# Weights alone on SyncE's queue, other transfers on GpSimd's, forms made in steps, layer-two gates kept on chip, last sums by transfers: a two-layer decoder trunk on one core

## The chip, the core and the metric

The kernel runs on one core of a Trainium2 chip. The core has five engines with queues of their own: TensorE (PE in the profile; its weight loads are PEld), VectorE (DVE), ScalarE (ACT), GpSimd (POOL) and SyncE (SP). Each executes its own instructions in order and waits for the others at semaphores. SyncE and GpSimd issue the DMA transfers here. The metric is the time of the program on the device in microseconds; the median of several runs counts.

## The reference

The input x has 512 rows (positions) of 2048 columns, in fp32. It passes two layers. Each is a token mixer with a gate, and then a residual sum with a LayerNorm.

```python
def fox_branch(x, w_in, b_f, q_gain, k_gain, w_out):          # layer 0, 16 heads of 128
    proj = jnp.einsum('bsd,de->bse', x, w_in)                 # 2048 -> 4*2048 + 16
    q, k, v, gate, f_logit = jnp.split(proj, [...], axis=-1)
    q = rms_norm(heads(q), q_gain); k = rms_norm(heads(k), k_gain); v = heads(v)
    c = jnp.cumsum(jax.nn.log_sigmoid(f_logit + b_f), axis=1).transpose(0, 2, 1)
    s = q k^T * scale + c[..., :, None] - c[..., None, :]     # causal, in blocks of 128 rows
    o = softmax(s) v
    return jnp.einsum('bse,ed->bsd', o * jax.nn.silu(gate), w_out)

def retention_branch(x, w_in, w_out):                         # layer 1, 8 heads, qk 256, v 512
    q, k, v, gate = jnp.split(jnp.einsum('bsd,de->bse', x, w_in), [...], axis=-1)
    q = rotary(q); k = rotary(k) * 256 ** -0.5
    o = (q k^T * decay) v                                     # written in the reference by chunks
    o = group_norm_heads(o)
    return jnp.einsum('bse,ed->bsd', o * jax.nn.silu(gate), w_out)

def reference(x, ...):
    h = x
    for i in range(2):
        y = fox_branch(...) if i % 2 == 0 else retention_branch(...)
        h = layer_norm(4.0 ** 0.25 * h + y, ln_gain[i], ln_bias[i])
    return h
```

## The kernel before

**Products.** All projections are products of a 512 x 2048 activation with slabs of weights: "narrow" slabs of 512 columns (q and k of two heads of layer one, or of one head of layer two) and "wide" ones of 1024 columns (gate and values, or half of an output projection). A `Unit` (L164) does one slab by a two-by-two scheme with seven products, p1 to p7, in place of eight. On the activation's side the products take seven *forms* (L40): the quarters a11, a12, a22 and the sums s1 to s4 of quarters. On the side of the weights they take quarters or running sums of quarters. Each fp32 operand is split into a high part (`w_h`, a rounded copy on ScalarE, L143) and a low part (`w_l`, the difference, on VectorE, L144), and `mm3` (L146 to 150) does three matmuls for one product.

**Blocks.** A weight quarter comes in blocks of 512 KB: two for a narrow unit, four for a wide one, so that a unit has 14 or 28 blocks in its seven products. For each block `run` (L263) loads it on SyncE (`load`, L181; tag `st`, three buffers, or a chain tile q0 to q3 that is kept), adds it to the chain or to another block where the product needs a sum (VectorE, L199 and L202), splits it (w_h and w_l have three buffers each), and queues the matmuls, which run two blocks behind the splits (`ahead`, `advance(2)`). `after` (L241) joins the products: it keeps p1, p5 and u2 in SBUF (tags k0 to k2) and hands four finished quarters to a `sink`.

**Work between blocks.** The mixers are lists of small steps in `pending` (L104). After the matmuls of each block `tick` runs one or more steps of that list, so that the heads of one unit are worked on between the blocks of the next. `finish_pending` runs all that is left at once. The order of the instructions on an engine follows their dependences and readiness, not strictly this text.

**Layer one.** `begin` (L285) does p1 and p2 of the first narrow and the first wide unit; meanwhile `form_of_x` and `combine` (L301) make the forms of x, all of them before `finish_pending` returns (L622). `forget` makes the cumulated logarithms. For each pair of heads: `scale` and `turn` (L473 to 496) normalise q and k, and for each head eight steps (L500 to 580): four row blocks of scores with a softmax (`cb`, the row of c, is loaded at L511), the transposes, `by_head` loads of values and gates (L538), mix, and gate. `give` (L344) then writes the head's result y, with signs by the table `GIVES`, into the forms of the output projection in DRAM: plain stores on SyncE (L356), accumulating transfers on GpSimd (L354). Heads 14 and 15 write their parts of the forms on chip (`last_heads`). `fetch_form` (L358) reads forms back and splits them, through the `st` buffers.

**The passage.** Units 4 and 5 are the output projection of layer one, the second in the order `EARLY`. `add_z` (L672) loads a block of x (tag tmp, four buffers, L83), adds and takes LayerNorm's statistics. `to_columns` (L715) normalises a row block, stores it (`z_norm`) and queues `turn` (L695), four transposes with gain and bias into the quarters of the new activation. After unit 5 the pipeline is drained (L735), the last turns are queued with `combine`, and `begin` starts layer two.

**Layer two.** Per head: `take_qk` copies q and k out, `attend` (L758) rotates them (two `cos_sin` tables, L768) and makes decayed scores (`dec`, L781), and two steps `residual` (L852) prepare alpha times the normalised row for later: three loads, two VectorE instructions, one store. `take_vg` (L795) writes the gate to DRAM (`rgates`, L607) and splits the values. `retain` (L804) queues mix, mix, norm, turn, turn twice: the mix reads the gate back (L816), the turn scales it (L832), transposes it (L835) and gives y and its negative to the forms.

**Output.** Units 14 and 15 add the first half of the output projection to the residual (`add_half`, L877: load, add, store), 16 and 17 the second; `store` (L896) does the last LayerNorm, every second column block with a sum on GpSimd (L904).

## Time and profile before

| | |
|---|---|
| Median of 3 runs | 2582.72 us (2579.68 to 2583.9) |
| The profiled execution's own time | 2578.53 us |
| Its span, from the first to the last instruction | 2576.8 us |
| Mean granted TensorE clock | 0.964 |
| Instructions | 34,299 |
| Read from HBM / written | 430.33 MB / 75.27 MB |

The profile is of one execution. A busy engine's row gives microseconds, share of the span and the number of instructions. A group's row gives line, engine, operation, what it writes and reads, shapes and count; then total busy time and the mean of one in ns; then the engine's idle time just before and what ended it. A row of waits names who waited at which line, for whom, with total us, count and the longest. A row of windows gives busy time and instructions of each engine, the clock granted to TensorE, the mean busy share of 16 DMA engines and GB/s. A row of issues gives the transfer, the issuing queue, the count, the size and the median us from issue to landing. `q0` is the queue of GpSimd's transfers, `q1` that of SyncE's.

### The profile page before, as it was taken

The numbers are of one execution on the slowest core, as the hardware profiler recorded it, in microseconds if no ns is written. First come the engines' busy times: TensorE is split into PE (matmuls) and PEld (weight loads), VectorE is DVE, ScalarE is ACT, GpSimd is POOL, SyncE is SP. The second block draws the span as 40 slices with busy tenths as digits, with TensorE's granted clock in tenths as the row PEclk, the third lists the DMA queues.
The fourth block names the chain that finished last, engine by engine and source line by source line (L and its number), as shares of the span: only waits on it lengthen the run. The fifth ranks groups of instructions, "written<-read, shape, count | busy, mean of one in ns | idle before, by whom it ended". The sixth has DMA issues, their size and how long they took to land.

```text
span 2576.8 us, 34299 instructions
## 1 busy us (share of the span) xinstructions
PE 2349.0 (91%) x12820; PEld 2001.7 (78%) x12820; DVE 2004.3 (78%) x2617; ACT 1276.9 (50%) x1891; POOL 100.8 (4%) x116
## 2 busy tenths in 40 slices
PE   6899999999997898699999999999999988897994
PEld 5788898898886687579797878788888866675773
DVE  7778687777776779887878878787878788577778
ACT  5456566666566445444454444444544444343432
POOL 0000000001101000000000000000000100100001
PEclk8999999999998999899999999999999999999997
DMA  6465746645755657467566566666676666677564
GB/s 243 156 217 168 235 150 172 217 160 159 221 190 162 217 188 269 155 196 208 178 220 194 193 191 202 181 203 189 208 212 201 190 198 216 191 241 241 193 213 147
DMA packets 213159, 507.86 MB, mean 197 GB/s; under 512 B 20080, under 2 KB 76784, under 8 KB 212736
## 3 DMA queue, kind: packets, MB, share of 16 engines
q1 hardware_dynamic: 198592, 485.22, 56.9%
q0 software_dynamic: 14400, 20.45, 5.6%
q8 instruction: 100, 1.64, 0.3%
q14 instruction: 67, 0.55, 0.1%
HBM read 430.33 MB, written 75.27 MB: 196 GB/s over the span
## 4 chain that ended last, share of the span: by engine, by line
PE 24%; DVE 14%; DMA 11%; issue 4%; ACT 4%; SPq 0%; POOL 0%; ACTq 0%; POOLq 0%; DVEq 0%
PE acc L149 7%; PE acc L150 7%; PE acc L148 7%; DVE w_l L144 5%; DMA w_raw<-in_wide 4%; ACT w_h L143 3%; DVE w_raw L202 2%; DMA w_raw<-in_narrow 2%; DMA y_s<-ny 1%; DMA cos_sin<-in_rot 1%; DMA ln_g<-in_ln_g 1%; DVE w_raw L199 1%; PE mmp L148 1%; DMA gate<-rgates 1%; DMA y_raw<-y_s 1%
## 5 line engine op out<-in xcount | busy, mean ns | idle before, releaser
L143 ACT ACTIVATE w_h<-w_raw 128x1024 fp32r<-128x1024 f32 x728 | 762.7, 1057 | 919.0 <-PE acc L150 277.0
L144 DVE TENSOR_TENSOR w_l<-w_raw,w_h 128x1024 fp32r<-128x1024 f32 x728 | 882.9, 1220 | 285.5 <-ACT w_h L143 281.1
L148 PE MATMUL acc<-w_h,s 128*128 128x512 f32 (+1 forms) x1664 | 607.7, 365 | 50.6 <-ACT w_h L143 46.6
L149 PE MATMUL acc<-w_l,s 128*128 128x512 f32 (+1 forms) x1664 | 609.2, 366 | 21.2 <-DVE w_l L144 20.4
L150 PE MATMUL acc<-w_h,s 128*128 128x512 f32 (+1 forms) x1664 | 602.6, 362 | 0.0
L148 PE MATMUL acc<-w_h,a 128*128 128x512 f32 (+1 forms) x1248 | 459.8, 369 | 47.3 <-ACT w_h L143 34.6
L149 PE MATMUL acc<-w_l,a 128*128 128x512 f32 (+1 forms) x1248 | 456.4, 366 | 33.8 <-DVE w_l L144 33.8
L150 PE MATMUL acc<-w_h,a 128*128 128x512 f32 (+1 forms) x1248 | 453.6, 363 | 0.0
L202 DVE TENSOR_TENSOR w_raw<-w_raw 128x1024 f32<-128x1024 f32 x312 | 378.5, 1218 | 69.8 <-DMA w_raw<-in_narrow 34.3
L148 PEld LDWEIGHTS acc<-w_h,s 128*128 128x128 f32 x1664 | 318.7, 192 | 108.3 <-ACT w_h L143 58.5
L149 PEld LDWEIGHTS acc<-w_l,s 128*128 128x128 f32 x1664 | 319.2, 192 | 84.2 <-DVE w_l L144 40.1
L150 PEld LDWEIGHTS acc<-w_h,s 128*128 128x128 f32 x1664 | 319.2, 192 | 43.5 <-DVE s L144 0.4
L148 PEld LDWEIGHTS acc<-w_h,a 128*128 128x128 f32 x1248 | 241.7, 194 | 91.9 <-ACT w_h L143 42.4
L149 PEld LDWEIGHTS acc<-w_l,a 128*128 128x128 f32 x1248 | 241.7, 194 | 72.4 <-DVE w_l L144 38.7
L150 PEld LDWEIGHTS acc<-w_h,a 128*128 128x128 f32 x1248 | 241.5, 194 | 35.0
L199 DVE TENSOR_TENSOR w_raw<-w_raw 128x1024 f32<-128x1024 f32 x104 | 126.9, 1220 | 51.1 <-DMA w_raw<-in_wide 39.8
L148 PE MATMUL acc<-s,w_h 128*128 128x256 f32 x512 | 145.9, 285 | 5.1 <-DVE u L255 2.0
L149 PE MATMUL acc<-s,w_h 128*128 128x256 f32 x512 | 146.1, 285 | 0.0
L150 PE MATMUL acc<-s,w_l 128*128 128x256 f32 x512 | 146.0, 285 | 0.0
L148 PE MATMUL acc<-a,w_h 128*128 128x256 f32 x384 | 110.8, 288 | 1.0 <-DVE p L258 1.0
L149 PE MATMUL acc<-a,w_h 128*128 128x256 f32 x384 | 110.1, 287 | 0.0
L150 PE MATMUL acc<-a,w_l 128*128 128x256 f32 x384 | 109.9, 286 | 0.0
(187 smaller groups left out, 2558.3 us busy)
## 6 DMA issues: line engine op xcount, KB each, us to landing
w_raw<-in_wide SPq DMA_DIRECT2D x468, 512.0 KB, 4.0
w_raw<-in_narrow SPq DMA_DIRECT2D x200, 512.0 KB, 3.6
y_raw<-y_s SPq DMA_DIRECT2D x35, 256.0 KB, 4.1
gate<-rgates SPq DMA_DIRECT2D x32, 256.0 KB, 4.6
y_s<-ny POOLq DMA_DIRECT2D x32, 256.0 KB, 7.5
y_raw<-y_a SPq DMA_DIRECT2D x26, 256.0 KB, 4.0
y_a<-y SPq DMA_DIRECT2D x24, 256.0 KB, 3.0
y_s<-y POOLq DMA_DIRECT2D x24, 256.0 KB, 7.0
```

What stands on the lines that cost most here:

```text
L143: nc.scalar.activation(h, src, AF.Copy)
L144: nc.vector.tensor_sub(l, src, f32(h))
L148: nc.tensor.matmul(ps, a[0], b[0], start=start, stop=False, skip_group_check=True)
L149: nc.tensor.matmul(ps, a[0], b[1], start=False, stop=False, skip_group_check=True)
L150: nc.tensor.matmul(ps, a[1], b[0], start=False, stop=stop, skip_group_check=True)
L199: nc.vector.tensor_add(t, t, b)
L202: nc.vector.tensor_add(self.chain[c], self.chain[c], t)
```

## The change

SyncE's queue keeps the weight loads, the loads of x at the start and the stores of the output. All other transfers are issued by GpSimd: `give`'s plain stores, `fetch_form`, `cb`, `by_head`, the stores of gates and values of layer one, `cos_sin`, `dec`, the residual's loads and stores, `z_norm`, and the blocks of z.

- Forms are made in single steps between blocks. A set `awaited` names forms that are not done; `multiply` runs pending steps until the form it needs is there. The first units start without draining the pipeline before them, the wide one first in layer two. x comes in smaller pieces.
- The gate of a layer-two head stays in SBUF (in the kept p1 and in k2) until the mix. The scaling moves from `turn` into `norm`, and the four turns follow after both norms.
- In the two units with the order EARLY, the sums of p7 and p4 are made by accumulating transfers into the tile of the other block, in place of VectorE's additions.
- z blocks of units 5, 15, 16 and 17 are loaded up to three ahead. The last sums of `store` are all VectorE's. Forms are fetched through tiles of their own (k2, k0, u; g2; in0 and in1).
- tmp has three buffers in place of four; the narrow unit keeps p1 and p5 in one tile (k1) and u2 in `u`. `scale` works on half of the rows at a time, p7's subtraction on halves, and one p2 block of unit 4 moves behind p3 and p7. Part of `to_columns` and `turn` goes from VectorE to ScalarE.

```diff
-        [(p, 3) for p in ("p5", "p6", "p2")] + blocks_of(4, ("p3", "p7"), ("p4",)))
+        [(p, 3) for p in ("p5", "p6")] + blocks_of(4, ("p3", "p7")) + [("p2", 3)] + blocks_of(4, ("p4",)))
...
-        return pool.tile([P, 512], F32, name=name, tag="tmp", bufs=4)
+        return pool.tile([P, 512], F32, name=name, tag="tmp", bufs=3)
...
+            if (p, c) in self.summed:
+                return self.summed.pop((p, c))
...
+        def add_by_transfer(self, p, c, q, t):
+
+            nc.gpsimd.dma_start(t.rearrange("p a b -> p (a b)"), self.w[self.n, int(q[1]) - 1, int(q[0]) - 1, c],
+                                accum_op=ALU.add)
+            self.summed[p, c] = t
...
         def multiply(self, p, c, w, streamed):
+            while FORM[p] in awaited:
+                pending.popleft()()
...
                 self.keep("p5", "z")
+                if self.early:
+
+                    for i in range(2):
+                        t = pool.tile([P, 2, 2, 512], F32, name="v_sum", tag=HOME["s1"][i])
+                        for c in range(2):
+                            nc.sync.dma_start(t[:, c].rearrange("p a b -> p (a b)"), self.w[self.n, 1, 0, 2 * i + c])
+                            self.add_by_transfer("p7", 2 * i + c, "22", t[:, c])
...
-                nc.vector.tensor_sub(k["p5"], k["p5"], b["x"])
+                for e in range(2):
+                    nc.vector.tensor_sub(k["p5"][:, e], k["p5"][:, e], b["x"][:, e])
...
                 split(raw, *w)
+                if self.early and p == "p6":
+                    self.add_by_transfer("p4", c, "21", self.chain[c])
...
-        for u in (first, second):
-            u.run(BEGIN, streamed=True)
+        for i, u in enumerate((second, first) if wide_first else (first, second)):
+            u.run(BEGIN, streamed=u is second, **{k: v[i] for k, v in kw.items()})
...
+        def step(name, c, make, last=True):
+            if c == 0 and name not in made:
+                made.add(name)
+                new_form(name)
+            make(c)
+            if c == 1 and last:
+                awaited.discard(name)
...
+        steps = [partial(step, "s1", c, s1) for c in range(2)] + [partial(step, "s2", c, s2) for c in range(2)]
+        steps.append(lambda: (s4_sum(0), s4_sum(1)))
+        for name, f in (("s4", s4), ("s3", s3), ("a22", a22)):
+            steps += [partial(step, name, c, f) for c in range(2)]
+        return steps
...
-                nc.sync.dma_start(d, y if sign > 0 else ny)
+                nc.gpsimd.dma_start(d, y if sign > 0 else ny)
...
-            t = pool.tile([P, n, 256], F32, name="y_raw", tag="st", bufs=3)
+            t = pool.tile([P, n, 256], F32, name="y_raw", tag=tag, **(dict(bufs=3) if tag == "st" else {}))
...
                 for e in range(2):
-                    nc.sync.dma_start(t[:, :, e * P:(e + 1) * P], yf[i][name][:, e, c:c + n])
+                    nc.gpsimd.dma_start(t[:, :, e * P:(e + 1) * P], yf[i][name][:, e, c:c + n])
...
-    form_of_x("11")
-    nothing = lambda: None
-    pending.extend([partial(form_of_x, "12"), nothing, nothing, nothing, quarters_of_x] + combine())
-    begin(qk[0], vg[0])
-    advance(0)
-    finish_pending()
...
+    first = iter([partial(form_of_x, "11", (0, 2, 4)), partial(form_of_x, "11", (4, 8)),
+                  partial(form_of_x, "12", (0, 4)), partial(form_of_x, "12", (4, 8))])
+    start = lambda: next(first)()
+
+    def combined():
+        pending.extend(combine() + [forget])
+
+    begin(qk[0], vg[0], before=({i: start for i in range(4)},
+                                {i: partial(quarter_of_x, *at) for i, at in enumerate(
+                                    (("21", 0), ("22", 0), ("21", 1), ("22", 1)))}),
+          then=({}, {2: combined}), spread=(0, 14))
...
-                nc.sync.dma_start(at["cb"], fox["rows"][head:head + 1, :].to_broadcast([P, S]))
+                nc.gpsimd.dma_start(at["cb"], fox["rows"][head:head + 1, :].to_broadcast([P, S]))
...
-                nc.sync.dma_start(t, src[head // 4][:, :, js])
+                nc.gpsimd.dma_start(t, src[head // 4][:, :, js])
...
+        def load():
+            if todo:
+                s, c = todo.popleft()
+                there.append(sb2("z_in"))
+                nc.gpsimd.dma_start(there[-1], src(s, c))
...
-    Unit(wide, 5, partial(add_z, 1, ALPHA, x_rows)).run(EARLY, then={"p3": first_half})
-    advance(0)
-    finish_pending()
-    to_columns(2)
-    to_columns(3)
-    new_quarters(1)
-    pending.extend(combine())
+    sink, load = add_z(1, ALPHA, x_rows, True, EARLY)
+    Unit(wide, 5, sink).run(EARLY, then={0: load, "p3": first_half, "p4": second_half})
...
-                        nc.sync.dma_start(cs[i], rot[i])
+                        nc.gpsimd.dma_start(cs[i], rot[i])
...
             if n == 0:
-                to_rows(rgates[self.h], True, m, tile)
+                self.gates[m] = tile if m == 0 else pool.tile([P, 2, 512], F32, name="gate", tag="k2")
+                silu_twice(self.gates[m], tile)
                 return
...
-                g[q] = sb2("gate")
-                nc.sync.dma_start(g[q], rgates[self.h][:, q])
...
+                for e in range(2):
+                    nc.scalar.activation(g[2 * i + e], g[2 * i + e], AF.Copy, scale=r[i][:, e:e + 1])
...
-                nc.scalar.activation(g[q], g[q], AF.Copy, scale=r[q // 2][:, q % 2:q % 2 + 1])
...
-                pending.extend([partial(mix, 2 * i), partial(mix, 2 * i + 1), partial(norm, i),
-                                partial(turn, 2 * i), partial(turn, 2 * i + 1)])
+                pending.extend([partial(mix, 2 * i), partial(mix, 2 * i + 1), partial(norm, i)])
+            pending.extend(partial(turn, q) for q in range(ST))
...
-        nc.sync.dma_start(t, z_norm[s][:, cs])
+        nc.gpsimd.dma_start(t, z_norm[s][:, cs])
...
-        nc.sync.dma_start(z_res[s, c], t)
+        nc.gpsimd.dma_start(z_res[s, c], t)
...
-        then = fetch_while(1) if h.h == RH - 1 else {}
+        then = fetch_while(1, ("g2",)) if h.h == RH - 1 else {}
...
-            if c % 2:
-                nc.scalar.activation(z, z, AF.Copy, scale=r)
-                nc.gpsimd.tensor_add(z, z, gb[1][:, cs])
-            else:
-                nc.vector.scalar_tensor_tensor(z, z, r, gb[1][:, cs], op0=ALU.mult, op1=ALU.add)
+            nc.vector.scalar_tensor_tensor(z, z, r, gb[1][:, cs], op0=ALU.mult, op1=ALU.add)
```

More of the change, by code (lines that the diff above doesn't have):

```diff
@@ L320, in s4 @@
[L320 to L332 removed]
+        sl = lambda c: (slice(None), slice(4 * c, 4 * c + 4))
@@ L804, in retain @@
         def retain(self):
-            mv, r, g = {}, {}, {}
+            mv, r = {}, {}
+            g = [self.gates[q // 2][:, q % 2] for q in range(ST)]
             def mix(q):
```

290 lines of the change are left out of this document (171 added, 119 removed).

## The prediction

> **What bounds the kernel now.** I read the head of the page first: the span, the busy time of each engine, the granted TensorE clock.
>
> ```profile
> span 2576.8 us, 34299 instructions
> PE 2349.0 (91%) x12820; PEld 2001.7 (78%) x12820; DVE 2004.3 (78%) x2617; ACT 1276.9 (50%) x1891; POOL 100.8 (4%) x116
> PEclk8999999999998999899999999999999999999997
> L143 ACT ACTIVATE w_h<-w_raw 128x1024 fp32r<-128x1024 f32 x728 | 762.7, 1057 | 919.0 <-PE acc L150 277.0
> L202 DVE TENSOR_TENSOR w_raw<-w_raw 128x1024 f32<-128x1024 f32 x312 | 378.5, 1218 | 69.8 <-DMA w_raw<-in_narrow 34.3
> ```
>
> TensorE is the bound: it idles 2576.8 - 2349.0 = 227.8 us, and no edit removes a product. So the change can win back idle time, and the clock that goes with it. The 728 splits count the weight blocks: 2576.8 / 728 = 3.54 us a block on average, mixers included. Next I cut the span into windows: start, layer one, the passage from layer one to two, the heads of layer two, the last output units, the tail.
>
> ```profile
> core 0: us, PE busy (x) PEld busy (x) DVE busy (x) ACT busy (x) POOL busy (x), PEclk, DMA share, GB/s
> 0.00:150.00 150.00, 122.65 (x714) 106.06 (x715) 114.15 (x140) 75.43 (x112) 1.09 (x8) 0.95 0.56 193
> 150.00:750.00 600.00, 593.94 (x3769) 527.15 (x3767) 458.93 (x671) 378.57 (x756) 31.71 (x36) 1.00 0.61 189
> 750.00:1110.00 360.00, 303.01 (x1536) 250.28 (x1537) 286.30 (x421) 188.09 (x312) 6.97 (x8) 0.92 0.61 197
> 1110.00:2050.00 940.00, 894.21 (x4972) 772.51 (x4971) 749.84 (x944) 426.78 (x498) 38.34 (x45) 0.98 0.65 199
> 2050.00:2557.00 507.00, 435.14 (x1837) 345.71 (x1835) 381.31 (x410) 205.34 (x212) 16.46 (x16) 0.94 0.66 209
> 2557.00:2577.00 20.00, 0.00 (x0) 0.00 (x0) 13.74 (x35) 2.67 (x4) 6.24 (x4) 0.60 0.27 105
> ```
>
> The TensorE idle times are 27.4, 6.1, 57.0, 45.8, 71.9 and 20.0 us. The clock is below 1 just where idle time lies, so a stall costs more than its length: (1 - clock) x busy is 6.1, 0, 24.2, 17.9 and 26.1 us. Per microsecond of idle time that makes 0.22, 0, 0.42, 0.39 and 0.36 more, and I let a recovered microsecond bring that along (an estimate: the clock need not follow in proportion).
>
> Third, who ended those waits. The rows come from the list of TensorE's waits, asked window by window (row 1 is of 0 to 150, rows 2 to 4 of 750 to 1110, rows 5 to 7 of 1110 to 2050, the last two from 2050 on).
>
> ```profile
> PE acc L149 <- DVE w_l L144: 12.0, 3, 6.2
> ...
> PE acc L149 <- DVE w_l L144: 20.3, 9, 15.6
> PE acc L148 <- DVE p L258: 9.2, 3, 6.0
> PE mmp L491 <- DVE qk_raw L484: 6.7, 2, 3.5
> ...
> PE mmp L835 <- ACT gate L832: 18.2, 11, 4.4
> PE acc L148 <- ACT w_h L143: 13.3, 14, 3.2
> PE acc L149 <- DVE w_l L144: 7.4, 13, 1.0
> ...
> PE acc L148 <- ACT w_h L143: 50.3, 22, 8.7
> PE acc L149 <- DVE w_l L144: 14.0, 14, 2.6
> ```
>
> TensorE rarely waits for a transfer by name; it waits for the two halves of a weight block, which VectorE and ScalarE made late, because they did something else or had no block. So the fourth view is SyncE's own waits, since every block comes through its queue.
>
> ```profile
> SPq L181 <- DVE w_l L144: 657.3, 281, 22.8
> SPq L181 <- DVE w_raw L202: 447.5, 165, 13.8
> SPq L861 <- DVE z_in L860: 45.8, 16, 6.2
> SPq L768 <- DMA y_s<-ny: 23.1, 11, 5.2
> ```
>
> The first two are a weight load waiting for its buffer: harmless pacing. The other two are stops for the stores of the residual and for the rotary tables, with weight loads queued behind: 69 us. The fifth view is GpSimd in one burst of accumulating transfers (the timeline), with one landing from the chain of waits.
>
> ```profile
> 1486.51 2.63 POOL L354 DMA_DIRECT2D y_s<-ny  x3 [18.30 <-ACT ny L841]
> 1491.86 0.87 POOL L354 DMA_DIRECT2D y_s<-ny  x1 [2.72 <-issue]
> 1494.43 0.85 POOL L354 DMA_DIRECT2D y_s<-ny  x1 [1.70 <-issue]
> 1497.28 0.86 POOL L354 DMA_DIRECT2D y_s<-ny  x1 [2.01 <-issue]
> ...
> 1487.61 9.36 DMA y_s<-ny
> ```
>
> Three go out at once, then each further one waits for no semaphore that the profile shows. The third lands at 1487.61 + 9.36 = 1496.97, and the sixth starts 0.31 us later. In this burst no more than three are under way, and the pace is (1497.28 - 1486.51) / 5 = 2.15 us an issue. This row matters most for the change: it puts nearly everything but weights on that queue.
>
> **Start (0 to 150): -9.5 us.** The first half of x's first quarter comes in two pieces, so the first split is half as long (1.06 to about 0.5 us by L143): -1 with its share of the load. The forms of x no longer run in one bunch ahead of the weight splits but one step per block. VectorE was busy 114 of 150, so it has room: of the 12.0 us wait I take 7, times 1.22 = 8.5. Bounds 0 and -15.6 (all 12.0, and the 1).
>
> **Layer one (150 to 750): +4 us.** There is nothing to win in 6.1 us. The loads of cb, by_head and the plain y_s writes move to GpSimd. Eight sums per head (heads 0 to 5), cb and two by_head loads are 11 issues, 24 us at 2.15; layer one has 600 / 14 = 43 us a head, but where a pair shares only the 14 blocks of a narrow unit, 14 x 3.54 / 2 = 25 us. VectorE already waits for cb on SyncE's queue:
>
> ```profile
> DVE cb L519 <- DMA cb<-c_rows: 12.0, 8, 2.9
> ```
>
> That is 1.5 us each, hidden by the three buffers of split weights (w_h, w_l), two blocks ahead, about 7 us. A cb that comes 5 us later eats that cover; without it, 6 heads of the three crowded pairs x 5 = 30 us. Bounds 0 and +30; I take 4, nearer to the covered end, as the average has room. tmp falls from 4 to 3 buffers, which delays by_head by one step, inside the same cover.
>
> **Passage (750 to 1110): -35.5 us.** Three edits act here. The ten forms become steps between the blocks of the next unit, which starts at once with products that need a11 and a12 only: 12 of the 20.3 us. Splitting the q/k scaling by rows and the p7 subtraction by halves, and moving the last p2 block behind p3/p7: 7 of the 9.2 + 6.7. In unit 5 transfers add 8 blocks, 8 x 1.218 = 9.7 us of VectorE, which is busy 286 of 360: 6. Together 25, times 1.42 = 35.5. Bounds -55 (39 of the 57.0 idle us) and -10 (7 us recovered), because the 80% busy VectorE still has to make the forms.
>
> What the adds cost in transfers, from the page's queue rows:
>
> ```profile
> q1 hardware_dynamic: 198592, 485.22, 56.9%
> q0 software_dynamic: 14400, 20.45, 5.6%
> y_s<-ny POOLq DMA_DIRECT2D x32, 256.0 KB, 7.5
> gate<-rgates SPq DMA_DIRECT2D x32, 256.0 KB, 4.6
> cos_sin<-in_rot SPq DMA_DIRECT2D x16, 256.0 KB, 6.3
> ```
>
> A megabyte takes 56.9 / 485.22 = 0.117% of 16 engines' span plain and 0.274% accumulating, 3.0 against 7.1 us. 4 MB a unit thus cost 16 us of transfer time more in about 100 us, where the share is 0.61: it stays under one, hidden, since the sums are issued a product ahead.
>
> **Heads of layer two (1110 to 2050): -8 us.** The gates stay in SBUF: 16 stores and 32 loads go (the rgates row), and the scaling moves out of the turn step, ahead of the transposes. The 18.2 us wait should fall to about 2: -16. Weight loads no longer stand behind tables and stores: half of 13.3 + 7.4, -10. Together 26 x 1.39 = -36.
>
> Against it stands the new queue. One head's turn steps now put all their y_s on GpSimd: 16 issues for heads 0, 1, 4, 5 and 12 for the others (counted in GIVES), 34 and 26 us at 2.15. Behind them stand cos_sin, then dec and the residual's three loads and store. The turns begin at the 7th pending item; rotate is about 8 blocks, 28 us, later. So cos_sin is issued 6 us late in four heads, and lands 6.3 us after that: VectorE stops in front of rope, with w_l of the coming blocks behind it, for 12 us, less the 7 us of cover: 5 x 4 = 20. ScalarE's y and ny also wait for one of three tmp buffers, with w_h splits behind: 8 heads x 1 = 8. Sum +28; bounds 0 (everything covered) and +70 (12 us on four heads, 5 on the others, tmp 2 to 3 on all). I take the value with the cover, as the same burst in the old kernel, with six of these issues, reached the chain of waits already.
>
> By the Trainium skill (DMA: Bandwidth & Descriptors, Anatomy of one DMA — SWDGE (gpsimd) path) such a transfer costs a fixed 2.0 us plus its bytes at 436 GB/s, 2.6 us for 256 KB as an estimate; this trace has 7.5, accumulating and in a burst. By the page the 28 us would be 0 and the sum 28 lower; I keep the row.
>
> **Output units (2050 to 2577): -30 us.** TensorE waits 50.3 + 14.0 here. z blocks are loaded three ahead, weights pass freely, unit 17 lets transfers add: half, 32 x 1.36 = -43.5. The tail's last sums go from GpSimd to VectorE: -1. Against it, 56 issues fetch forms for the two output layers and 48 move z blocks on GpSimd: 104 x 2.15 = 224 us of 507, room on average; but forms come in bunches of four to eight, some behind one single buffer (g2): +14, bounds 0 and +60.
>
> **Sum.** -9.5 + 4 - 35.5 - 8 - 30 = -79. The profiled execution took 2578.5 us (its span and 1.7 around it), which gives 2499.5; the median shown is 2582.7, 4.2 more: **2504 us**.
>
> **Rivals.** *A, the queue split buys nothing.* SyncE's great waits (657.3 and 447.5) are for buffers that VectorE frees; a queue that waits for its consumer isn't helped by company leaving. Then the gains of freer weight loads (10 x 1.39 = 14 and 43.5) fall away and the costs stay: 2504 + 57 = **2561**. Against it: the 69 us in which other stops held loads back. The Trainium skill says the same (DMA: Bandwidth & Descriptors, Issuing engines are not separate DMA queues): issuing from several engines saves only issue time. The trace doesn't quite agree, by those 69 us.
>
> *B, slower: three in flight on GpSimd decide.* About 520 issues at 2.15 are 1120 us; place: cos_sin behind the turn bursts, and the form fetches. If bursts outrun the 7 us of cover everywhere, the three bounds hold: +26 in layer one, +42 in layer two, +46 at the end beyond what I have: 2504 + 114 = **2618**. It decides once a load that VectorE or ScalarE needs stands behind more than three to four transfers. For it: the "issue" gaps. Against: most plain transfers should land sooner than 9.36 us, and the average load is under a half.
>
> *C, more: covers hold and stalls vanish.* Costs 0, start -15, passage -55, layer two -36, end -60 (44 of the 71.9 idle us, times 1.36): 2578.5 - 166 + 4.2 = **2417**. Against it: VectorE at 80% in the passage.
>
> *D, no effect*, because VectorE's own work sets the pace throughout: within 0.2%. Its 573 us of idle time speak against.
>
> **How the numbers follow.** Forecast 0.36 (own range 2465 to 2545), A 0.19, B 0.23, C 0.18, D 0.04. Outside 2420 to 2615 I leave half of C and half of B, 2 in 10. About 0.2% is what a measurement here tells from no change. Faster: forecast, A less a sliver, C: 0.72; within 0.2%: 0.05; slower: 0.23.
>
> **What would show it.** Right: TensorE idle near 17, 8, 35, 35 and 45 us in the five stages; the wait for the gate scaling near 2 us; SyncE's waits for anything but buffers of weights gone; the long w_l wait of the passage (15.6 us) below 5. Wrong: GpSimd's issues with waits of 2 us and more in front all through; VectorE waiting for cos_sin, cb or ln_g by tens of us; ScalarE's y or ny waiting for y_s to land. If layer one loses more than 30 us, B was the right reading.

## The result: the changed kernel is slower

The changed kernel takes 2708.85 us (median of 4 runs, 2700.49 to 2709.94) against 2581.2 us before (2578.3 to 2583.9): a ratio of 1.0488, 95% interval 1.0463 to 1.0512. The forecast of 2504 us fails in direction, and 2708.85 lies above its range of 2420 to 2615.

The head of the page of the changed kernel:

```profile
span 2706.9 us, 34279 instructions
PE 2388.0 (88%) x12820; PEld 2026.9 (75%) x12820; DVE 1989.3 (73%) x2732; ACT 1275.7 (47%) x1896; POOL 343.2 (13%) x530
...
PE   7999999999987888999999999999999765967885
...
PEclk9999999999999899999999999999999887988987
...
q1 hardware_dynamic: 96912, 348.17, 38.4%
q0 software_dynamic: 49776, 138.63, 19.1%
```

The 12,820 products are the same. The span is 130.1 us longer: TensorE idles 318.9 us in place of 227.8 (91 more), and the same products take 39 us more, at a mean granted clock of 0.948 in place of 0.964. GpSimd's queue q0 now carries 138.63 MB in place of 20.45. The sixteen DMA engines are not fuller for it: 38.4 + 19.1 = 57.5% here, 62.5% before. In the 40 slices the hole lies from slice 32 on, in the output units. The windows are those of the prediction up to 2050, then the rest:

```profile
core 0: us, PE busy (x) PEld busy (x) DVE busy (x) ACT busy (x) POOL busy (x), PEclk, DMA share, GB/s
0.00:150.00 150.00, 129.89 (x759) 111.58 (x760) 125.48 (x166) 79.39 (x118) 5.50 (x16) 0.98 0.61 210
150.00:750.00 600.00, 576.64 (x3596) 509.18 (x3595) 442.57 (x708) 361.61 (x733) 89.18 (x131) 0.99 0.58 178
750.00:1110.00 360.00, 301.78 (x1559) 250.53 (x1558) 269.39 (x433) 197.22 (x331) 46.48 (x72) 0.93 0.59 186
1110.00:2050.00 940.00, 882.14 (x4826) 759.99 (x4826) 739.73 (x920) 417.87 (x484) 101.73 (x163) 0.98 0.59 183
2050.00:2600.00 550.00, 430.64 (x1827) 343.25 (x1826) 344.64 (x392) 194.83 (x208) 89.65 (x133) 0.89 0.55 169
2600.00:2707.00 107.00, 66.88 (x265) 52.38 (x263) 67.51 (x117) 24.78 (x24) 10.66 (x15) 0.81 0.58 179
```

TensorE idles 20.1, 23.4, 58.2 and 57.9 us in the first four, and 119.4 + 40.1 = 159.5 in the rest, where it was 71.9 + 20.0. Fixed windows slide over the work once a kernel is longer, so I also measured the stages by their own work: from the start of the first `w_h` split of one unit to that of the next (728 splits in each kernel, counted out by blocks).

```
us, split to split        before   after   difference   predicted
start (to vg 0)            158.1   146.0     -12.1         -9.5
layer one (qk 1 to 7)      608.8   647.0     +38.2         +4
passage (4, 5, begin)      282.4   268.2     -14.2        -35.5
heads of layer two         998.2  1019.1     +20.9         -8
units 13 to 17, tail       522.2   618.2     +96.0        -30
```

The borders lie near those of the prediction's windows but not on them: 165, 774, 1056 and 2054 us in the old kernel, against 150, 750, 1110 and 2050. Layer one and the passage are best read together (+24): steps that wait in `pending` slide over the border between them.

What holds up the output units? First GpSimd, whose issues the timeline of the changed kernel shows:

```profile
2389.19 0.76 POOL L422 DMA_DIRECT2D y_raw<-y_a  x1 [4.22 <-issue]
2393.04 0.75 POOL L422 DMA_DIRECT2D y_raw<-y_s  x1 [3.08 <-issue]
2397.11 0.76 POOL L422 DMA_DIRECT2D y_raw<-y_s  x1 [3.32 <-issue]
2402.03 0.75 POOL L422 DMA_DIRECT2D y_raw<-y_s  x1 [4.17 <-issue]
2406.16 0.76 POOL L422 DMA_DIRECT2D y_raw<-y_s  x1 [3.38 <-issue]
2410.51 0.75 POOL L422 DMA_DIRECT2D y_raw<-y_s  x1 [3.59 <-issue]
2414.41 0.76 POOL L422 DMA_DIRECT2D y_raw<-y_s  x1 [3.15 <-issue]
```

These are form fetches (`fetch_form`). The engine stands idle 3 to 4 us before each and waits for no semaphore that the profile shows. The pace is (2414.41 - 2389.19) / 6 = 4.20 us a fetch, and the page gives 4.0 us from issue to landing for `y_raw<-y_s`: they go one at a time. The starts and landings in the trace say the same of all 56 fetches of the two output layers: none starts while another is under way, and each of the 39 nameless waits before them ends 0.30 to 0.37 us after the landing of a transfer from GpSimd. The lists of waits of GpSimd (first row) and ScalarE (the next two), and the same two rows of the old kernel:

```profile
POOL y_raw L422 <- issue: 142.5, 39, 6.3
...
ACT s L143 <- DMA y_raw<-y_s: 109.4, 17, 11.2
ACT a L143 <- DMA y_raw<-y_a: 76.9, 12, 17.8
```

```profile
ACT s L143 <- DMA y_raw<-y_s: 26.5, 12, 8.3
...
ACT a L143 <- DMA y_raw<-y_a: 6.2, 5, 2.8
```

ScalarE, which splits forms and weight blocks in one order, waits 186 us for fetched forms where it waited 33, and the weight splits stand behind.

### The profile page after: what moved, and what is told of

It reads as the page before. It is cut to its first block, busy times and chain, and to the rows that moved or that the text cites. A ratio compares the mean times of both kernels' runs of the same rounds, so it can differ in the third digit from the quotient of the medians.

```text
span 2706.9 us, 34279 instructions
## 1 busy us (share of the span) xinstructions
PE 2388.0 (88%) x12820; PEld 2026.9 (75%) x12820; DVE 1989.3 (73%) x2732; ACT 1275.7 (47%) x1896; POOL 343.2 (13%) x530
## 3 DMA queue, kind: packets, MB, share of 16 engines
q1 hardware_dynamic: 96912, 348.17, 38.4%
q0 software_dynamic: 49776, 138.63, 19.1%
## 5 line engine op out<-in xcount | busy, mean ns | idle before, releaser
L143 ACT ACTIVATE w_h<-w_raw 128x1024 fp32r<-128x1024 f32 x720 | 753.6, 1056 | 869.1 <-DVE w_raw L207 302.0
L144 DVE TENSOR_TENSOR w_l<-w_raw,w_h 128x1024 fp32r<-128x1024 f32 x720 | 872.4, 1220 | 288.2 <-ACT w_h L143 284.0
L149 PE MATMUL acc<-w_l,s 128*128 128x512 f32 (+1 forms) x1664 | 614.0, 369 | 32.9 <-DVE w_l L144 32.4
L148 PE MATMUL acc<-w_h,a 128*128 128x512 f32 (+1 forms) x1248 | 465.6, 373 | 65.2 <-ACT w_h L143 42.8
L149 PE MATMUL acc<-w_l,a 128*128 128x512 f32 (+1 forms) x1248 | 461.4, 370 | 22.4 <-DVE w_l L144 22.3
L150 PE MATMUL acc<-w_h,a 128*128 128x512 f32 (+1 forms) x1248 | 458.0, 367 | 0.0
L148 PEld LDWEIGHTS acc<-w_h,s 128*128 128x128 f32 x1664 | 323.4, 194 | 137.3 <-ACT w_h L143 61.0
L207 DVE TENSOR_TENSOR w_raw<-w_raw 128x1024 f32<-128x1024 f32 x304 | 368.9, 1218 | 65.7 <-DMA w_raw<-in_wide 51.0
L149 PEld LDWEIGHTS acc<-w_l,s 128*128 128x128 f32 x1664 | 323.0, 194 | 95.4 <-DVE w_l L144 50.8
L150 PEld LDWEIGHTS acc<-w_h,s 128*128 128x128 f32 x1664 | 323.1, 194 | 45.8 <-DVE s L144 0.7
L148 PEld LDWEIGHTS acc<-w_h,a 128*128 128x128 f32 x1248 | 244.6, 196 | 113.0 <-ACT w_h L143 50.6
L149 PEld LDWEIGHTS acc<-w_l,a 128*128 128x128 f32 x1248 | 244.6, 196 | 65.3 <-DVE w_l L144 31.6
L150 PEld LDWEIGHTS acc<-w_h,a 128*128 128x128 f32 x1248 | 244.2, 196 | 35.5
L149 PE MATMUL acc<-s,w_h 128*128 128x256 f32 x512 | 144.8, 283 | 0.0
L204 DVE TENSOR_TENSOR w_raw<-w_raw 128x1024 f32<-128x1024 f32 x96 | 117.1, 1219 | 22.8 <-DMA w_raw<-in_wide 14.2
L148 PE MATMUL acc<-a,w_h 128*128 128x256 f32 x384 | 114.9, 299 | 14.2 <-ACT w_h L143 11.6
L149 PE MATMUL acc<-a,w_h 128*128 128x256 f32 x384 | 113.4, 295 | 0.0
```

Of the source, the lines that this page charges most:

```text
L143: nc.scalar.activation(h, src, AF.Copy)
L144: nc.vector.tensor_sub(l, src, f32(h))
L148: nc.tensor.matmul(ps, a[0], b[0], start=start, stop=False, skip_group_check=True)
L149: nc.tensor.matmul(ps, a[0], b[1], start=False, stop=False, skip_group_check=True)
L150: nc.tensor.matmul(ps, a[1], b[0], start=False, stop=stop, skip_group_check=True)
L204: nc.vector.tensor_add(t, t, b)
```

## The experiments

**Theories.** Theory Q: GpSimd's queue holds only so much, and the form fetches, each in many small pieces, stall on it; all else is secondary. The first rival: the tiles through which forms are fetched (one g2, in0, in1) are the limit, whatever the queue. The second: many small costs on GpSimd, of which the fetches are one. Each ratio below is to the old kernel, measured beside that run, with its 95% interval in brackets; times of stages are from split to split.

### Form fetches on SyncE; fetches in larger pieces

```diff
 fetch_form, e1:
-                nc.gpsimd.dma_start(t, yf[i][name][sl])
+                nc.sync.dma_start(t, yf[i][name][sl])
-                    nc.gpsimd.dma_start(t[:, :, e * P:(e + 1) * P], yf[i][name][:, e, c:c + n])
+                    nc.sync.dma_start(t[:, :, e * P:(e + 1) * P], yf[i][name][:, e, c:c + n])
```

> The changed kernel with the fetches of forms alone back on SyncE's queue (their tiles g2, in0, in1, k2, k0, u stay). Theory Q (the queue): GpSimd's queue holds only so many pieces of transfers, a fetch of 512 pieces of 512 bytes fills it, so the 56 fetches of the two output layers go one by one, about 4.3 us each, and that makes the 86 us by which the units from head 7's wide one to unit 15 grew. Then this kernel takes 2709 - 85 = 2624 us, within 20. Theory T (the tiles): the one buffer g2 and the pair in0/in1 in place of three st buffers make it; then it stays above 2680. Theory W (the waits of the other moved transfers): the same, above 2680.

Measured: 2595.7 us, ratio 1.0053 [1.0034, 1.0073]. That is 113 us back, more than the 85 that Q expected. By stages 110 of it lies where it was lost: units 13 to 17 take 508.4 us (618.2 with the fetches on GpSimd).

The second leaves the fetches on GpSimd and changes only their shape: the tile is filled in the order of DRAM, so that, by the code, 256 KB go as 128 pieces of 2 KB in place of 512 pieces of 512 B, and the split reads it through a view.

```diff
...
+                r = t.rearrange("p k (e s) -> p (k e s)", e=2).rearrange("p (e k s) -> p e k s", e=2, k=n)
                 for e in range(2):
-                    nc.gpsimd.dma_start(t[:, :, e * P:(e + 1) * P], yf[i][name][:, e, c:c + n])
-            split_form(name, t, sl)
+                    nc.gpsimd.dma_start(r[:, e], yf[i][name][:, e, c:c + n])
+                h, l = (f[sl].rearrange("p k (e s) -> p e k s", e=2) for f in forms[name])
+                split(r, h, l)
```

> The changed kernel with the form fetches of the two output layers still on GpSimd's queue and of the same bytes and number, but each in 128 pieces of 2 KB: the tile takes DRAM's order and the splits read it through a view. Theory Q: several then are under way at once, the issue gaps in front of them (142.5 us) nearly vanish, and 40 to 70 us come back: 2640 to 2670, less than with SyncE, since g2 still serves one piece at a time. Theory T or W: 2695 to 2709.

Measured: 2600.81 us, ratio 1.0073 [1.0051, 1.0095], again more than expected; units 13 to 17 take 513.3 us. Its timeline on GpSimd, and from the list of its waits the row of ScalarE:

```profile
2335.19 1.07 POOL L424 DMA_DIRECT2D y_raw<-y_s  x2 [3.96 <-DVE a L144]
2338.59 1.07 POOL L424 DMA_DIRECT2D y_raw<-y_s  x2 [2.33 <-DVE s L144]
2342.81 1.07 POOL L424 DMA_DIRECT2D y_raw<-y_s  x2 [3.15 <-DVE s L144]
```

```profile
ACT s L143 <- DMA y_raw<-y_s: 54.3, 18, 9.9
```

The two halves of a fetch now go out back to back (x2), and what the engine waits for has a name: the split that frees the tile. Same bytes, same queue, same tiles, 108 us less: the pieces decide, and the tiles as the main cause fall. The page's row of q0 counts 49,776 packets in both kernels, so it doesn't show the pieces; the issuing instruction does, with 0.75 us each for 512 pieces and 0.54 for 128.

### The same loss made in the old kernel

```diff
 before, fetch_form:
-                nc.sync.dma_start(t, yf[i][name][sl])
+                nc.gpsimd.dma_start(t, yf[i][name][sl])
...
-                    nc.sync.dma_start(t[:, :, e * P:(e + 1) * P], yf[i][name][:, e, c:c + n])
+                    nc.gpsimd.dma_start(t[:, :, e * P:(e + 1) * P], yf[i][name][:, e, c:c + n])
```

> The kernel before with one part of the change alone: its form fetches on GpSimd's queue, still through the three st buffers. Theory Q: the fetches go one by one and delay splits, and through st the weight loads too: 2581 + 40 to 100. Theory T: within 10 us of 2581.

Measured: 2689.7 us, ratio 1.0420 [1.0395, 1.0445]: 109 us lost by this edit alone, a little more than expected, with three `st` buffers to fetch through. All of it lies in units 13 to 17 (632.5 us, 522.2 before). The waits of GpSimd and of TensorE, the latter 81.2 us in the old kernel:

```profile
POOL y_raw L370 <- issue: 153.9, 42, 5.9
...
PE acc L148 <- ACT w_h L143: 140.8, 39, 21.9
```

The chain is whole: GpSimd can't issue, ScalarE waits for a form, TensorE for the high half of a weight block.

### What is full: the store of descriptors

If pieces decide, something that is counted in pieces is full. The launch sets aside a scratch space for GpSimd's transfers (`dynamic_dma_scratch_size`), 1024 bytes in both kernels; theory Q takes it for the store of the descriptors, one or more for each piece, of transfers under way. To double it, room in SBUF has to be freed. So the control first frees 2 KB in the kernel above, without enlarging anything: tmp with three buffers, `forget`'s rows in g2.

```diff
 control (from the old kernel with its fetches on GpSimd):
-        return pool.tile([P, 512], F32, name=name, tag="tmp", bufs=4)
+        return pool.tile([P, 512], F32, name=name, tag="tmp", bufs=3)
-        f, a, u, c = nf("f"), nf("a"), nf("u"), nf("c")
+        rows = sb8("fg", "g2")[:FH]
+        f, a, u, c = (rows[:, i] for i in range(4))
 and then, on top of the control:
-    nc = bacc.Bacc("TRN2", ..., dynamic_dma_scratch_size=1024)
+    nc = bacc.Bacc("TRN2", ..., dynamic_dma_scratch_size=2048)
```

> A control: the kernel before with its form fetches on GpSimd (2690 us), tmp with three buffers and forget's rows in another tile, which frees 2 KB a partition that nothing uses. Expected 2690 to 2705 by every theory.

> The control with one number changed: 2048 in place of 1024 bytes a partition for the descriptors of GpSimd's transfers (dynamic_dma_scratch_size). Theory Q in its strict form, the store of descriptors is what a 512-piece fetch fills: two fetches are then under way at once, the issue gaps before them (153.9 us) fall by more than half, and the kernel is 40 to 80 us faster than the control, 2615 to 2660. Rival (GpSimd's transfers of small pieces are slow each, whatever the store): no difference over 10 us.

Measured: 2706.7 us (1.0485 [1.0464, 1.0506]) for the control, 2606.01 us (1.0086 [1.0062, 1.0110]) with 2048 bytes: 101 us from that one number, 97 of them in units 13 to 17 (633.0 and 536.2 us). The waits of GpSimd and ScalarE, first the control, then with the larger store, and the timeline of the latter:

```profile
POOL y_raw L370 <- issue: 160.0, 45, 6.0
...
ACT s L143 <- DMA y_raw<-y_s: 103.1, 19, 7.8
```

```profile
POOL y_raw L370 <- issue: 17.2, 11, 3.2
...
ACT s L143 <- DMA y_raw<-y_s: 39.3, 18, 6.2
```

```profile
2357.22 1.49 POOL L370 DMA_DIRECT2D y_raw<-y_s  x2 [19.37 <-DVE w_raw L199]
2360.45 0.76 POOL L370 DMA_DIRECT2D y_raw<-y_s  x1 [1.74 <-DVE w_l L144]
2361.67 0.75 POOL L370 DMA_DIRECT2D y_raw<-y_s  x1 [0.46 <-issue]
2362.66 0.75 POOL L370 DMA_DIRECT2D y_raw<-y_s  x1 [0.25 <-issue]
```

Twice the store, and up to three 512-piece fetches are under way, where in the control none of the 56 starts beside another. The first two of these rows land at 2361.36 and 2362.14, so the fetch at 2360.45 goes out beside them, and the one at 2361.67 follows the first landing by 0.31 us. The nameless wait falls from 160.0 to 17.2 us. A fetch by itself is no quicker: its median from issue to landing is 4.3 us, 3.8 in the control. So the rival that transfers of small pieces are merely slow falls too. The Trainium skill (DMA: Bandwidth & Descriptors, SWDGE vs HWDGE vs iDMA) says that GpSimd appends descriptors to rings in a carved-out part of SBUF; the runs fit that, and add that its size can be the bound. That the scratch space is this part is theory Q's reading; what the runs show is that its size, and the number of pieces, decide how many transfers are under way. The changed kernel itself wasn't tried with 2048 bytes, for want of room in SBUF.

The control is also 17 us slower than the kernel it comes from, 14 of them in the heads of layer two (1007.0 against 993.1 from split to split). `forget` runs only in layer one, so that is most likely the price of the fourth tmp buffer. It isn't a fixed one: with 2048 bytes and the same three buffers the heads take 999.8 us.

### What the other moved transfers cost

All plain transfers back on SyncE; only accumulating ones stay on GpSimd (every plain `nc.gpsimd.dma_start` becomes `nc.sync.dma_start`):

> The changed kernel with every plain transfer back on SyncE; GpSimd issues only the accumulating ones, as before, and the 16 sums of units 5 and 17. Theory Q and W together: all that the queue split cost comes back, 85 at the end, 25 in the narrow units of layer two, 25 in layer one: about 2575. If the split did help the weights elsewhere (the rival of the prediction's forecast), this gives that up, and it comes out above the kernel with the forms alone on SyncE.

Measured: 2542.6 us, ratio 0.9858 [0.9828, 0.9888]: faster than before, and than expected. Its head of the page, and its window of the passage:

```profile
span 2538.4 us, 34294 instructions
PE 2339.9 (92%) x12820; PEld 1998.5 (79%) x12820; DVE 1990.2 (78%) x2732; ACT 1278.2 (50%) x1896; POOL 102.2 (4%) x124
```

```profile
750.00:1110.00 360.00, 307.89 (x1567) 254.57 (x1567) 277.94 (x424) 197.33 (x324) 13.93 (x16) 0.94 0.62 194
```

TensorE idles 198.5 us, 29 less than before. Of the loss, form fetches are 113 us and all other plain transfers 53 (2595.7 - 2542.6), so the second rival holds for a third of what the moved transfers cost. To see which, single kinds went back to SyncE on top of the first experiment (form fetches there already). The plain y stores of `give`:

```diff
-                nc.gpsimd.dma_start(d, y if sign > 0 else ny)
+                nc.sync.dma_start(d, y if sign > 0 else ny)
```

> The kernel with the forms alone back on SyncE (2596 us), with the plain y_s stores of the heads on SyncE too. The prediction put 28 us (bound 70) on these bursts: cos_sin and the residual's loads behind 12 or 16 issues, and ScalarE's y and ny waiting for tmp. If so, the narrow units of layer two (55 to 57 us each) come back to about 52 and the whole falls by 20 to 30 us, to 2566 to 2576. If the bursts don't matter, it stays within 5 us.

Measured: 2576.45 us (0.9989 [0.9976, 1.0002]), 19 us less, just short of the expected 20 to 30. The place was only in part the expected one: 8 us come in the heads of layer two, 11 in layer one and the passage. ScalarE's wait for y's stores, with the plain stores on GpSimd (first) and on SyncE:

```profile
ACT ny L947 <- DMA y_s<-y: 44.3, 16, 6.3
```

```profile
ACT ny L947 <- DMA y_s<-y: 27.5, 10, 5.9
```

`cb` and `by_head` of layer one:

```diff
-                    nc.gpsimd.dma_start(at["cb"], fox["rows"][head:head + 1, :].to_broadcast([P, S]))
+                    nc.sync.dma_start(at["cb"], fox["rows"][head:head + 1, :].to_broadcast([P, S]))
-                nc.gpsimd.dma_start(t, src[head // 4][:, :, js])
+                nc.sync.dma_start(t, src[head // 4][:, :, js])
```

> The kernel with the forms alone back on SyncE (2596 us), with the loads of cb and by_head of layer one on SyncE too. by_head is another load of 512 pieces of 512 bytes. Theory Q: it goes alone as well, late for TensorE, which waits for by_head by name (9 us); units vg2, vg3 and qk7 lose 15 to 25 us of their excess, 2571 to 2581. Rival (three tmp buffers in place of four delay the heads, whatever the queue): within 5 us of 2596.

Measured: 2595.7 us (1.0059 [1.0043, 1.0076]), no change. Theory Q's own expectation fell here: by the code `by_head` too is a load of 512 pieces, and in the trace no two of its loads are under way together, yet moving it brings nothing. So a transfer that goes alone need not cost time. That it costs where many follow each other and ScalarE needs each at once is the likely reading, argued from the form fetches. On top of the y stores, the rotary tables, the decay and the residual's transfers of layer two:

```diff
-                        nc.gpsimd.dma_start(cs[i], rot[i])
+                        nc.sync.dma_start(cs[i], rot[i])
...
-        nc.gpsimd.dma_start(t, z_norm[s][:, cs])
+        nc.sync.dma_start(t, z_norm[s][:, cs])
...
-        nc.gpsimd.dma_start(z_res[s, c], t)
+        nc.sync.dma_start(z_res[s, c], t)
```

> The changed kernel with form fetches, plain y stores, and now also the rotary tables, the decay, and the residual's three loads and one store of layer two on SyncE; values, gates, cb, by_head and the z blocks stay on GpSimd. With the y stores moved too, the kernel took 2576 us (its heads of layer two 1009 us from split to split); with every plain transfer on SyncE 2543 (heads 988). If the tables and the residual's loads behind the accumulating bursts are what is left of the loss in layer two, as the prediction's term for cos_sin has it: heads of layer two near 990, median about 2556. Rival, no one kind decides but SyncE's queue as a whole: heads stay above 1003, median 2570 or more.

Measured: 2557.78 us (0.9917 [0.9898, 0.9936]), 19 us less, as expected in time. VectorE's waits with these loads on GpSimd, then on SyncE:

```profile
DVE z_in L966 <- DMA ln_b<-in_ln_b: 23.8, 14, 2.5
DVE rope L876 <- DMA cos_sin<-in_rot: 21.7, 7, 5.4
```

```profile
DVE z_in L966 <- DMA ln_b<-in_ln_b: 13.0, 14, 1.6
DVE rope L876 <- DMA cos_sin<-in_rot: 6.2, 3, 3.1
```

The heads of layer two fall from 1009.4 to 999.0 us, not to the 990 expected; another 11 us go only when the rest goes too (987.7), and which of the rest carries them stays open. The blocks of z, put back on GpSimd alone on top of the version with all plain transfers on SyncE (loads, `z_half`, the last gains):

```diff
-                nc.sync.dma_start(there[-1], src(s, c))
+                nc.gpsimd.dma_start(there[-1], src(s, c))
...
-                nc.sync.dma_start(z_half[2 * m + e, 2 * u + n], t)
+                nc.gpsimd.dma_start(z_half[2 * m + e, 2 * u + n], t)
...
```

> The kernel with all plain transfers on SyncE, except that the z blocks of units 4, 5 and 14 to 17, the stores of z_half and z_res and the last gains are GpSimd's, as in the changed kernel. Theory Q (only transfers of many pieces and bursts hurt on GpSimd's queue; single ones that wait for VectorE are well placed there, as they stop no weight load): 5 to 15 us faster than 2543, in the last four units. If any moved transfer loses: slower than 2543.

Measured: 2540.23 us (0.9851 [0.9833, 0.9868]), no difference to 2542.6: with the fetches away, z blocks on either queue cost the same.

### What the other parts of the change gain

All these start from the version with all plain transfers on SyncE. Gates of layer two through DRAM again, scaled in `turn`:

```diff
-                self.gates[m] = tile if m == 0 else pool.tile([P, 2, 512], F32, name="gate", tag="k2")
-                silu_twice(self.gates[m], tile)
+                to_rows(rgates[self.h], True, m, tile)
...
+                g[q] = sb2("gate")
+                nc.sync.dma_start(g[q], rgates[self.h][:, q])
...
```

> The kernel with all plain transfers on SyncE (2543 us), with one more part undone: the gates of layer two go through DRAM again, the scaling stands in the turn step, and the turns follow each norm, as before. The prediction priced this part at 16 us of idle time, 22 with the clock: then 2560 to 2570, with TensorE's wait for the gate scaling back at about 18 us. If the heads of layer two were hidden anyway, it stays within 5 us of 2543.

Measured: 2573.53 us (0.9969 [0.9951, 0.9988]), 31 us more, and TensorE's old wait is back:

```profile
PE mmp L941 <- ACT gate L938: 18.7, 11, 3.4
```

So the gates on chip, with the scaling in `norm` and the turns after both norms, gain about 31 us, somewhat more than expected. Sums by transfers left out altogether (VectorE adds, as before):

```diff
 after p5:
-                if self.early:
-                    for i in range(2):
-                        t = pool.tile([P, 2, 2, 512], F32, name="v_sum", tag=HOME["s1"][i])
...
 after p6's splits:
-                if self.early and p == "p6":
-                    self.add_by_transfer("p4", c, "21", self.chain[c])
```

> The kernel with all plain transfers on SyncE (2543 us), with one more part undone: the p7 and p4 sums of units 5 and 17 are VectorE's additions again. If the sums by transfers pay (9.7 us of VectorE a unit, taken as 6 in the prediction), this is 8 to 15 us slower than 2543, in units 5 and 17. If an accumulating 512 KB block, which takes 11 us to land, comes late, it is 5 to 15 us faster, and unit 5 falls from 105 back to about 96 us.

Measured: 2542.44 us (0.9852 [0.9832, 0.9871]), the same. The next run mixed two things: z_res and z_half on SyncE but the other z blocks and last gains on GpSimd, and the sums in unit 17 alone.

```diff
...
-            self.early = order is EARLY
+            self.early = order is EARLY and self.n == 17
...
```

> A version meant to be the fastest: the kernel with z blocks on GpSimd (2540 us), but units 14 and 15 move theirs on SyncE (unit 15 took 84.8 us so, 99.2 with GpSimd), and sums by transfers only in unit 17 (without them unit 5 took 95 in place of 105 us, with them unit 17 took 5 less). Theory Q adds these up: 2540 - 14 - 10 = 2516, within 12. If the units only trade stalls with their neighbours, 2530 to 2545.

Measured: 2547.78 us (0.9861 [0.9839, 0.9883]); this expectation fell. The stages tell why the sums came to nothing: with them the passage takes 261.4 us and units 16 and 17 with the tail 215.9, without them 265.9 and 207.3. They gain in unit 5 and lose in unit 17. The mixed run, with sums in unit 17 alone, agrees: 265.5 and 214.4. So the sums in unit 5 alone:

```diff
-            self.early = order is EARLY
+            self.early = order is EARLY and self.n == 5
```

> All plain transfers on SyncE, sums by transfers only in unit 5, VectorE adds again in unit 17. Without any sums by transfers the passage (units 4, 5 and the two begins) took 265.9 against 261.4 us and units 16 and 17 with the tail 207.3 against 215.9. If these two differences are the sums' own, both are kept here: passage 261, last two units 207, median about 2534. Rival, they are scatter from trace to trace: median 2540 to 2545.

Measured: **2532.16 us**, ratio 0.9816 [0.9797, 0.9836], with 261.2 and 207.1 us in the two stages. It is the fastest version measured, 10 us below the one it comes from (the intervals of the two ratios overlap a little). Last, the q/k scaling in one step again:

```diff
...
-            pending.extend([partial(scale, 0), partial(scale, 1)] + [partial(turn, s) for s in range(ST)])
+            pending.extend([scale] + [partial(turn, s) for s in range(ST)])
```

> All plain transfers on SyncE, and the q/k scaling of layer one again in one step over all four row blocks. Layer one takes 628.9 us with all plain transfers on SyncE and 608.8 before. If the halves cost (a second chain of 12 small VectorE instructions in each of 8 pairs, in front of the w_l of the coming blocks): layer one 615 to 620, median about 2532. Rival, the excess comes from the three tmp buffers in place of four or from the narrow unit's shared tile: layer one stays at 627 to 630, median 2540 to 2545.

Measured: 2539.7 us (0.9845 [0.9824, 0.9865]), no sure gain. Layer one does fall, to 615.5 us, but the passage rises to 275.5: the sum is 891.0, where the halves make 890.3 (and the old kernel 891.2). The expected gain moved over the border between the stages.

## Why the prediction was wrong

**The step that failed** is the term of the output units for moved transfers: "+14, bounds 0 and +60". It took its pace, 2.15 us an issue, from accumulating transfers, and read that row as a limit of three transfers under way. A form fetch goes alone, at 4.20 us, because two fetches of 512 pieces don't fit together into a store that holds three accumulating transfers. The cost is 110 us in these stages, nearly twice the upper bound. The code showed the pieces (`t[:, :, e * P:(e + 1) * P]`, 128 of every 256 columns), and no row of the old trace showed such a transfer on GpSimd's queue; a bound from that trace had to allow one at a time, at the 4 us that a fetch took there from issue to landing on SyncE's queue.

This step alone is 96 of the 205 us between forecast and measurement. With the form fetches on SyncE the kernel takes 2595.7 us, still slower than before: the other moved transfers cost 53 us more, and the gains of the passage and the output units came out smaller, as follows.

**Rival B had the mechanism**, a full GpSimd queue ahead of loads that VectorE and ScalarE need, and named the form fetches. It priced them at +46 beyond the forecast where they cost about 96, so its 2618 us is also too low. Its threshold, "more than three to four transfers", was a count of transfers; the runs with larger pieces and with the larger store point to a count of pieces.

**Start**, predicted -9.5: -12.1. Right, and by the mechanism named for most of it: in the first 150 us TensorE waits 1.0 us for `w_l` at L149 in place of 12.0.

**Layer one**, +4 with bounds 0 and +30: +38.2. The signal that the prediction set (more than 30 us lost here: B was right) came. With all plain transfers on SyncE +20 is left, which belongs to the account of the next stage: layer one and the passage together lose 24 us in the changed kernel and nothing in that version.

**Passage**, -35.5: -14.2. The one long wait is gone from its line, but another for `w_l` stands at the next, as the list of TensorE's waits from 750 to 1125 shows:

```profile
PE acc L150 <- DVE w_l L144: 10.9, 3, 8.3
PE acc L149 <- DVE w_l L144: 9.5, 7, 4.2
```

The longest was 15.6 us, and the prediction asked for less than 5; it is 8.3 now. And the time is not saved: TensorE idles 58.2 us from 750 to 1110, 57.0 before, and layer one and the passage together take 890.3 us even with all plain transfers on SyncE, 891.2 before, and the first unit of layer two 43.2 where it took 34.2. VectorE stays busy for 277.94 of these 360 us with all plain transfers on SyncE; it was 286.30 before. The likely reading, not tested by a run of its own, is that the forms made in steps push VectorE's work into the neighbouring units; the step that fails by it is to count a named wait of TensorE as time to be won while the engine behind it has the same work to do.

**Heads of layer two**, -8: +20.9. Two of the terms had the right sign and order of size. The gates: 22 us predicted (16 x 1.39), 31 measured. The bursts in front of cos_sin and the residual: 20 predicted; from 1017.4 us (form fetches on SyncE) to 987.7 (all plain ones there) it is 30, of which y stores, tables and the residual's transfers make 18.5. Not seen is the gain of 14 from freer weight loads. The fourth tmp buffer may cost up to 14 by the control, where the prediction put 8; no run tests it in the changed kernel.

**Freer weight loads.** SyncE's waits in the changed kernel:

```profile
SPq L184 <- DVE w_l L144: 1047.5, 321, 29.7
SPq L184 <- DVE w_raw L207: 689.4, 187, 20.4
```

The stops for tables and stores are gone, as predicted, and the waits for buffers grew from 657.3 and 447.5 us: the queue stands longer before the same buffers. That fits rival A, though part of it goes with the longer kernel. What speaks most plainly against the split is that the version with all plain transfers on SyncE, weights among them, is 53 us faster than the one with form fetches alone there.

**Output units without the fetches**, -43.5 - 1 predicted: -13.8 with form fetches on SyncE, -23.8 with sums in unit 5 alone. The direction was right, the size not; sums by transfers in unit 17, counted there as a gain, cost 8 to 9 us.

## What to carry to other kernels

Before moving transfers to GpSimd's queue, count their pieces and not their bytes: a transfer in many small pieces can fill the queue's store by itself, and then the next waits until it has landed. Where waits named "issue" stand in front of DMA issues and end just after a landing, look at that store; larger pieces, a larger store or SyncE's queue each took 100 us and more away here. And a change of several parts is worth taking apart: under a loss of 5% lay 31 us for gates on chip, and the best mix is 1.8% faster than the old kernel.

## What the runs showed of the hardware that was not expected

- The same 256 KB on the same queue cost 108 us more over the kernel as 512 pieces than as 128 (56 fetches), and 101 us went away with a store of 2048 bytes in place of 1024.
- By the starts and landings in the traces, with 1024 bytes at most one fetch of 512 pieces, or six plain transfers of 128 pieces, was under way, and at most three accumulating ones; with 2048 bytes, up to three fetches and six accumulating ones.
- A plain transfer from GpSimd landed 4.0 us after its issue (256 KB, form fetches), and the 512 KB accumulating loads of weights after 10.9, by the changed kernel's rows of issues; accumulating ones of 256 KB in bursts took 7.5 in the old kernel:

```profile
y_raw<-y_s POOLq DMA_DIRECT2D x35, 256.0 KB, 4.0
...
w_raw<-in_wide POOLq DMA_DIRECT2D x8, 512.0 KB, 10.9
```

- Idle time came with a lower granted clock (0.89 in the 550 us from 2050 on) and with longer products, but in no fixed proportion. In the changed kernel 91 us more idle time went with 39 us more of TensorE's busy time. In the old kernel with its form fetches on GpSimd, 90 us more went with 19, at a mean clock of 0.942. The prediction's share of 0.36 for this stage is thus not a constant.
